# Two heads in one PSUM bank: both casts first, then both subtractions

## The chip, the cores and the metric

The kernel runs on one core of one Trainium2 chip. The metric is the time of one execution on the device in microseconds (us), less is better. The engines of the core work from queues of their own, each in its own order: TensorE (PE, matrix products and transposes), VectorE (DVE), ScalarE (ACT), GpSimd (POOL) and SyncE (SP, which here issues transfers). PSUM is the memory that TensorE writes its results to, in eight banks of 512 fp32 columns by 128 rows.

## The reference

One decoder layer on x of 1024 tokens by 1024 features. Two groups of eight heads (64 wide) read one input projection: group A with a sliding window of 128, two key heads, ALiBi and sinks; group B with forget gates over all earlier tokens. Then an output projection with a residual, and an MLP with squared ReLU.

```python
xn = rmsnorm(x, attn_norm_g)
proj = jnp.einsum('bsd,de->bse', xn, w_in)
qa, ka, va, qb, kb, vb, f_logit = jnp.split(proj, IN_SPLITS, axis=-1)
qa = rmsnorm(qa.reshape(b, s, A_HEADS, HEAD_DIM), q_norm_a)     # ka, qb, kb alike
out_a = swa_sinks_attention(qa, ka, va, sink_logits)
log_f = jax.nn.log_sigmoid(f_logit + b_forget)
out_b = forgetting_attention(qb, kb, vb, log_f)
x = x + jnp.einsum('bse,ed->bsd', mixed, w_out)
hid = jnp.square(jax.nn.relu(jnp.einsum('bsd,df->bsf', rmsnorm(x, mlp_norm_g), w_up)))
x = x + jnp.einsum('bsf,fd->bsd', hid, w_down)
```

## The kernel before, in words

Products are made from numbers split in two parts. A high part is the number cast to the matmul's shorter fp32 form (type fp32r), a low part is what the cast left over; a product is then the sum of two or three passes. Usually ScalarE casts the high part, and VectorE or GpSimd subtracts to get the low part.

*Stages.* Up to about 45 us x and the first weights are loaded and split, and the first projection runs (tile qps). From 45 to 200 us follow the other projections of group A (tile ps) and group A's attention; from there to about 430 us group B's four pairs of heads, with the next pair's projection (ps) or the first half of the output projection (tile po) as filler between the attention's small products. Then the output projection ends, and the MLP takes the rest: the up products (pu) to about 770 us, the down products (pd) to the end.

*Turned banks.* Projected and normalised queries and keys lie with tokens along the rows. `turn` (line 327) transposes four blocks of 128 tokens on TensorE into one PSUM bank (tiles ptq for queries, ptk for keys, from a ring of three banks that the probabilities' transposes, tpa and tpb, share). The bank then holds head features along the rows: two heads, one in rows 0 to 63 and the other in rows 64 to 127. `rows_of` gives each head's rows.

From the bank, each head's part is made into high and low parts:

- Queries: `q_split` (lines 321 to 325) has ScalarE cast with a gain (line 322) and VectorE multiply and subtract (line 323). The high part goes to the head's own rows of q1a or q1b, the low part to the other 64 rows of the same tile. `make_q_a` (line 347) serves group A, `make_q_b` (line 355) group B, both head by head.
- Keys: `k_split` (lines 369 to 376) has ScalarE copy the high part twice, to both row halves of k1a or k1b (lines 371 and 372), and VectorE make the low part k2z (line 374), for group A twice. `make_k_a` (line 380) does this for the two key heads in one bank, `make_k_b` (line 388) for one head at a time.

*Who reads them.* Scores (`scores_a`, `scores_b`) are TensorE products of q1a or q1b with k1 and then k2z, into tiles sp and spb (two banks in turn). VectorE adds the bias and takes the row minimum (lines 543 and 717), ScalarE the exponential (lines 550 and 722). Probabilities are transposed (lines 564 and 762), split by ScalarE and VectorE (lines 401 and 402), and multiplied with the values (pv, pvb). The mix is added up (lines 575 and 780) and stored by SP.

*Other work on the same queues.* ScalarE also copies finished projections out of PSUM (lines 458, 459 and 646, from a ring of two banks) and casts weights (line 76). VectorE also multiplies earlier mixes with their inverse sums (line 623), once a transfer has brought these.

*The order of the work.* The source gives dependencies and priorities; `prep` raises the priority of the attention's steps over the filler. The kernel is built with

```python
with tile.TileContext(nc, schedule_with_timeline_sim=True) as tc:
```

so a planner works out, from modelled times, the order in which each engine gets its instructions, and adds the waits between engines. 
Of the kernel before, what the change touches and what calls it, by code (L numbers as in the profile page):

```python
# [8 lines left out]
F32 = mybir.dt.float32  # L9
F32R = mybir.dt.float32r  # L10
BF16 = mybir.dt.bfloat16
AF = mybir.ActivationFunctionType
ALU = mybir.AluOpType
# [8 lines left out]
HD = 64  # L22
# [32 lines left out]
def hybrid_layer(  # L55
# [13 lines left out]
    nc = tc.nc  # L69
# [11 lines left out]
    def rsqrt(pool, out, t, shape, tag):  # L81
# [15 lines left out]
        out=ident, in_=ident, pattern=[[-1, P]], compare_op=ALU.not_equal,  # L97
# [12 lines left out]
    gqk = cp.tile([P, 2], F32, name="gqk")  # L110
# [42 lines left out]
    def x_part(j, k, rows):  # L153

        c, r0 = divmod(rows.start, 512)
        return X[c][k // 2][:, j, k % 2, r0 : r0 + rows.stop - rows.start]
# [27 lines left out]
    for k in range(KT):  # L184
# [18 lines left out]
        for cs in pieces:  # L203
            hi, lo = (x_part(j, k, cs) for j in range(2))
            nc.scalar.activation(hi, xr[:, cs], AF.Copy, scale=ga)
            last_x = nc.vector.scalar_tensor_tensor(  # L206
                out=lo, in0=xr[:, cs], scalar=ga,
                in1=hi.bitcast(F32), op0=ALU.mult, op1=ALU.subtract,
# [109 lines left out]
        )  # L318
        return v

    def q_split(hi, lo, src, gain):
        nc.scalar.activation(hi, src, AF.Copy, scale=gain)
        nc.vector.scalar_tensor_tensor(
            out=lo, in0=src, scalar=gain, in1=hi.bitcast(F32), op0=ALU.mult, op1=ALU.subtract
        )

    def turn(x, col, w, c, name):
        pt = pa.tile([P, 512], F32, tag="tr", name=name, bufs=3)
        for j in range(4):
            nc.tensor.transpose(  # L330
                pt[:w, j * P : (j + 1) * P], x[:, 4 * c + j, col : col + w], ident
            )
        return pt
# [7 lines left out]
    rows_of = [slice(h * HD, (h + 1) * HD) for h in range(2)]  # L341
# [5 lines left out]
    def make_q_a(g, c, j):  # L347
        x, col = (((q0, 0), (q3, 0)), ((q3, P), (q3, 2 * P)))[g][j]
        q1 = qa[g, j, c]
        pt = turn(x, col, P, c, "ptq")  # L350
        for h in range(2):
            r, ro = rows_of[h], rows_of[1 - h]
            q_split(q1[r, h, :], q1[ro, h, :], pt[r, :], gqk[r, 0:1])

    def make_q_b(x, p):
        q1 = [ap2.tile([P, S], F32R, tag="q1", name=f"q1b{p}{h}", bufs=4) for h in range(2)]
        for c in range(2):
            cs = slice(c * 512, (c + 1) * 512)
            pt = turn(x, 0, P, c, "ptq")
            for h in range(2):  # L360
                r, ro = rows_of[h], rows_of[1 - h]
                q_split(q1[h][r, cs], q1[h][ro, cs], pt[r, :], gqk[r, 1:2])
        return q1

    k2_of = [ap2.tile([P, S], F32R, name=f"k2z{i}") for i in range(2)]

    def k_split(k1, i, src, cs, both):
        r, ro = rows_of[i], rows_of[1 - i]  # L370
        nc.scalar.copy(k1[r, cs], src)
        nc.scalar.copy(k1[ro, cs], src)
        for rr in (r, ro) if both else (r,):
            nc.vector.tensor_tensor(
                out=k2_of[i][rr, cs], in0=src, in1=k1[r, cs].bitcast(F32), op=ALU.subtract
            )

    k1a = {}

    def make_k_a(x, col, c):  # L380
        cs = slice(c * 512, (c + 1) * 512)
        pt = turn(x, col, P, c, "ptk")
        for g in range(2):
            if c == 0:
                k1a[g] = ap2.tile([P, S], F32R, tag="k1", name=f"k1a{g}", bufs=2)
            k_split(k1a[g], g, pt[rows_of[g], :], cs, True)

    def make_k_b(x, col, p, h):
        k1 = ap2.tile([P, S], F32R, tag="k1", name=f"k1b{p}{h}", bufs=2)
        if p == 0:  # L390
            nc.gpsimd.memset(k2_of[h][rows_of[1 - h], :].bitcast(F32), 0.0)
        for c in range(2):
            cs = slice(c * 512, (c + 1) * 512)
            pt = turn(x, col + h * HD, HD, c, "ptk")
            k_split(k1, h, pt[:HD, :], cs, False)
        return k1

    def evict_pt(pt, cols):
# [11 lines left out]
    for t in range(NT):  # L410
# [4 lines left out]
        out=rt, in0=rt, scalar1=1.0 / D, scalar2=EPS, op0=ALU.mult, op1=ALU.add  # L415
# [6 lines left out]
    for t in range(0, NT, 4):  # L422
# [8 lines left out]
        out=dist, in_=dist, pattern=[[-1, 256]], compare_op=ALU.is_ge, fill=BIG,  # L431
# [3 lines left out]
        out=dist, in_=dist, pattern=[[1, 256]], compare_op=ALU.is_ge, fill=BIG,  # L435
# [8 lines left out]
    for pattern, base, sign in (  # L444
# [5 lines left out]
            out=before, in_=before, pattern=pattern, compare_op=ALU.is_ge, fill=0.0,  # L450
# [58 lines left out]
    def start_a():  # L509
        for c in range(2):  # L510
            tiles_q_a(0, c)
        for t in range(2):
            wa1_tile(t)
        for c in range(2):
            wa1_tile(2 + c)
            with tc.issue_after(middle[-1]):
                prep(make_k_a, q0, P, c)
            prep(make_q_a, 0, c, 0)
        for g in range(2):
            va.append(split_v(q0[:, :, 256 + g * HD : 256 + (g + 1) * HD], f"va{g}"))  # L520
        prep(make_q_a, 0, 0, 1)
        for t in range(4, NT):
            wa1_tile(t)
        prep(make_q_a, 0, 1, 1)
# [130 lines left out]
    def prep_q(p):  # L655
        heads[p, "q"] = make_q_b(qkb[p], p)

    def prep_k(p, h):
        heads[p, "k1", h] = make_k_b(qkb[p], P, p, h)
        if h == 0:  # L660
            load_c(p, 0)
# [343 lines left out]
    rr = o["zr"].tile([P, S], F32, name="rr")  # L1005
# [231 lines left out]
    queued, both = [], []  # L1237
# [175 lines left out]
    for i in range(len(STEPS)):  # L1413
        down(i)
        if STEPS[i][0] == len(PHASES) - 1 and late:
            name, dt, cs = late.pop(0)
# [65 lines left out]
```

## Time and profile before

| | |
|---|---|
| three runs, median | 1080.25 us (1079.21 to 1080.84) |
| the profiled execution's own time | 1080.32 us |
| its span, first to last instruction | 1078.6 us |
| TensorE busy | 1069.6 us, 99% |
| VectorE busy | 774.6 us, 72% |
| ScalarE busy | 575.6 us, 53% |
| GpSimd busy | 382.0 us, 35% |
| granted TensorE clock | 1.000 |

The span leaves out 1.72 us of the execution's time around the first and last instruction. Busy shares are means over all stages. A wait in the profile is given with the instruction that ended it: "PE sp L72 <- DVE q1a L323" reads: TensorE stood before its product into sp, called at line 72, until VectorE had written q1a at line 323. The `mm` helper makes all products at line 72, so they are told apart by their tiles.

### The profile page before, as it was taken

What the parts mean: (1) busy time and instruction counts of PE and PEld (TensorE: products, weight loads), DVE (VectorE), ACT (ScalarE), POOL (GpSimd) and SP (SyncE); (2) the same over time, 40 slices, a digit from 0 to 9 for tenths busy, and PEclk for the clock granted to TensorE, in tenths of its full rate; (3) what the DMA queues carried; (4) which work ended last, traced back from release to release, by engine and by line L of the source; (5) the groups of instructions that cost most, each with busy time, mean ns of one, the idle gap of its engine ahead of it and who ended that gap; (6) DMA issues with size and microseconds to landing.
All of it is one profiled execution on the core that took longest, in us unless ns stands there. A gap on an engine that the chain in (4) does not pass through costs nothing.

```text
span 1078.6 us, 15605 instructions
## 1 busy us (share of the span) xinstructions
PE 1069.6 (99%) x5506; PEld 931.9 (86%) x5506; DVE 774.6 (72%) x1319; ACT 575.6 (53%) x1024; POOL 382.0 (35%) x347
## 2 busy tenths in 40 slices
PE   9999999999999999999999999999999999999998
PEld 8999999999998888888888888888888888888887
DVE  7377787777775777997877869674775876764395
ACT  5558587777666765555445454534533433333331
POOL 5572423546456663333233322332212313231100
PEclk9999999999999999999999999999999999999999
DMA  9402111424657665645554543443998886665423
GB/s 285 169 16 60 61 44 57 122 79 148 224 192 241 218 226 217 205 156 176 185 175 178 178 173 120 178 162 117 372 391 308 306 294 207 243 220 184 172 92 117
DMA packets 96366, 195.93 MB, mean 182 GB/s; under 512 B 7408, under 2 KB 19872, under 8 KB 96288
## 3 DMA queue, kind: packets, MB, share of 16 engines
q1 hardware_dynamic: 96000, 194.80, 52.0%
q8 instruction: 43, 0.70, 0.3%
q14 instruction: 35, 0.29, 0.1%
q10 hardware_dynamic: 288, 0.15, 0.0%
HBM read 141.87 MB, written 53.04 MB: 181 GB/s over the span
## 4 chain that ended last, share of the span: by engine, by line
PE 90%; DVE 3%; DMA 2%; ACT 2%; POOL 1%; issue 1%; SPq 0%; DVEq 0%; ACTq 0%; POOLq 0%
PE pu L72 28%; PE pd L72 28%; PE ps L72 12%; PE po L72 8%; PE spb L72 3%; PE pvb L72 3%; PE tpb L762 2%; PE sp L72 1%; PE pv L72 1%; PE tpa L564 1%; DMA xq<-in_x_dram 1%; DVE x L206 1%; PE ptk L330 1%; DMA wr<-in_w_a_dram 1%; PE ptq L330 0%
## 5 line engine op out<-in xcount | busy, mean ns | idle before, releaser
L72 PE MATMUL pd<-hx,wx 128*128 128x512 f32 (+1 forms) x1356 | 305.0, 387 | 0.0
L72 PEld LDWEIGHTS pd<-hx,wx 128*128 128x128 f32 x1356 | 253.1, 188 | 51.9
L72 PE MATMUL pu<-bh,wu 128*128 128x512 f32 x896 | 276.1, 389 | 0.0
L72 PE MATMUL ps<-w,x 128*128 128x384 f32 (+1 forms) x960 | 198.5, 343 | 0.8 <-ACT qkb L646 0.5
L72 PEld LDWEIGHTS pu<-bh,wu 128*128 128x128 f32 x896 | 168.2, 188 | 34.9
L72 PE MATMUL pu<-bl,wu 128*128 128x512 f32 x448 | 174.1, 389 | 0.0
L72 PEld LDWEIGHTS ps<-w,x 128*128 128x128 f32 x960 | 165.3, 188 | 5.1 <-ACT qkb L646 0.7
L76 ACT CAST hx<-hr 128x1024 fp32r<-128x1024 f32 x56 | 59.1, 1054 | 175.8 <-PE pd L72 171.1
L79 POOL TENSOR_TENSOR wx<-wda,wx 128x1024 fp32r<-128x1024 f32 x24 | 65.6, 2731 | 195.4 <-ACT wx L76 168.9
L79 DVE TENSOR_TENSOR hx<-hr,hx 128x1024 fp32r<-128x1024 f32 x56 | 72.3, 1300 | 71.5 <-ACT hx L76 71.5
L72 PEld LDWEIGHTS pu<-bl,wu 128*128 128x128 f32 x448 | 84.1, 188 | 17.6
L72 PE MATMUL po<-mix,wos 128*128 128x512 f32 x384 | 94.4, 394 | 0.1
L79 POOL TENSOR_TENSOR wu<-wus,wu 128x512 fp32r<-128x512 f32 x31 | 44.8, 1447 | 112.4 <-ACT wu L76 112.4
L72 PEld LDWEIGHTS po<-mix,wos 128*128 128x128 f32 x384 | 70.7, 188 | 14.0 <-ACT pc L950 0.3
L79 POOL TENSOR_TENSOR wu<-wur,wu 128x512 fp32r<-128x512 f32 x31 | 44.8, 1447 | 98.8 <-ACT wu L76 84.5
L76 ACT CAST wu<-wus 128x512 fp32r<-128x512 f32 x64 | 38.4, 618 | 62.8 <-PE pu L72 55.9
L1071 DVE TENSOR_TENSOR ht<-hb 128x512 f32<-128x512 f32 x32 | 21.7, 720 | 59.4 <-ACT hb L1182 59.4
L76 ACT CAST wx<-wda 128x1024 fp32r<-128x1024 f32 x56 | 58.5, 1049 | 7.2 <-DMA wda<-in_w_d_dram 7.2
L402 DVE TENSOR_TENSOR ptl<-tpb,pth 128x512 fp32r<-128x512 f32 (+1 forms) x80 | 49.7, 632 | 15.1 <-ACT pth L401 14.5
L722 ACT ACTIVATE sb<-sb,nmb 128x128 f32<-128x128 f32 (+3 forms) x64 | 49.8, 778 | 19.7 <-DVE nmb L717 19.1
L79 POOL TENSOR_TENSOR w<-wr,w 128x384 fp32r<-128x384 f32 (+1 forms) x47 | 50.1, 1078 | 27.7 <-ACT w L76 15.0
L401 ACT CAST pth<-tpb 128x512 fp32r<-128x512 f32 (+1 forms) x80 | 42.3, 544 | 14.3 <-PE pvb L72 6.2
(211 smaller groups left out, 1789.1 us busy)
## 6 DMA issues: line engine op xcount, KB each, us to landing
wda<-in_w_d_dram SPq DMA_DIRECT2D x34, 1024.0 KB, 9.1
hr<-hid_d SPq DMA_DIRECT2D x56, 512.0 KB, 6.3
wur<-in_w_u_dram SPq DMA_DIRECT2D x32, 512.0 KB, 4.4
hid_d<-ht SPq DMA_DIRECT2D x16, 1024.0 KB, 4.3
hid_d<-hb SPq DMA_DIRECT2D x16, 768.0 KB, 3.8
mix<-mixs_d SPq DMA_DIRECT2D x7, 1024.0 KB, 6.2
wr<-in_w_b_dram SPq DMA_DIRECT2D x32, 192.0 KB, 2.4
xq<-in_x_dram SPq DMA_DIRECT2D x8, 512.0 KB, 5.7
```

The source lines that it names most:

```text
L72: return nc.tensor.matmul(out, lhsT, rhs, start=start, stop=stop)
L76: hi_eng.copy(hi, src)
L79: return lo_eng.tensor_tensor(out=lo, in0=src, in1=hi.bitcast(F32), op=ALU.subtract)
L206: last_x = nc.vector.scalar_tensor_tensor(out=lo, in0=xr[:, cs], scalar=ga, in1=hi.bitcast(F32), op0=ALU.mult, op1=ALU.subtract,)
L330: nc.tensor.transpose(pt[:w, j * P : (j + 1) * P], x[:, 4 * c + j, col : col + w], ident)
L401: nc.scalar.copy(hi[:, cols], pt[:, cols])
L402: nc.vector.tensor_tensor(out=lo[:, cols], in0=pt[:, cols], in1=hi[:, cols].bitcast(F32), op=ALU.subtract)
L564: nc.tensor.transpose(tp[:, hh * P : (hh + 1) * P], pts[hh // 2][:, hh % 2, c0 : c0 + P], ident)
L722: nc.scalar.activation(pr[:, :nk], pr[:, :nk], AF.Exp, scale=-1.0, bias=nm[:, c : c + 1], accum_out=dn_b[p % 2][:, h, i : i + 1] if p < 3 ...
L762: nc.tensor.transpose(tp[:, c0 : c0 + P], probs[qi][:, kb * P : (kb + 1) * P], ident)
L1071: eng.tensor_tensor(out=out, in0=a, in1=b, op=ALU.subtract)
```

## The change

Both queries' and keys' helpers take all heads of a bank at once. ScalarE's casts of all heads come first in the source, then VectorE's subtractions of all heads. What each instruction reads and writes stays the same.

```diff
-    def q_split(hi, lo, src, gain):
-        nc.scalar.activation(hi, src, AF.Copy, scale=gain)
-        nc.vector.scalar_tensor_tensor(
-            out=lo, in0=src, scalar=gain, in1=hi.bitcast(F32), op0=ALU.mult, op1=ALU.subtract
-        )
+    def q_splits(pt, gain, plane):
+
+        rr = [(rows_of[h], rows_of[1 - h]) for h in range(2)]
+        for h, (r, _) in enumerate(rr):
+            nc.scalar.activation(plane(h)[r], pt[r, :], AF.Copy, scale=gain[r])
+        for h, (r, ro) in enumerate(rr):
+            nc.vector.scalar_tensor_tensor(
+                out=plane(h)[ro], in0=pt[r, :], scalar=gain[r],
+                in1=plane(h)[r].bitcast(F32), op0=ALU.mult, op1=ALU.subtract,
+            )
...
     def make_q_a(g, c, j):
...
-        for h in range(2):
-            r, ro = rows_of[h], rows_of[1 - h]
-            q_split(q1[r, h, :], q1[ro, h, :], pt[r, :], gqk[r, 0:1])
+        q_splits(pt, gqk[:, 0:1], lambda h: q1[:, h, :])
...
     def make_q_b(x, p):
...
-            for h in range(2):
-                r, ro = rows_of[h], rows_of[1 - h]
-                q_split(q1[h][r, cs], q1[h][ro, cs], pt[r, :], gqk[r, 1:2])
+            q_splits(pt, gqk[:, 1:2], lambda h: q1[h][:, cs])
...
-    def k_split(k1, i, src, cs, both):
-        r, ro = rows_of[i], rows_of[1 - i]
-        nc.scalar.copy(k1[r, cs], src)
-        nc.scalar.copy(k1[ro, cs], src)
-        for rr in (r, ro) if both else (r,):
-            nc.vector.tensor_tensor(
-                out=k2_of[i][rr, cs], in0=src, in1=k1[r, cs].bitcast(F32), op=ALU.subtract
-            )
+    def k_splits(parts, cs, both):
+        for k1, i, src in parts:
+            for rr in rows_of[i], rows_of[1 - i]:
+                nc.scalar.copy(k1[rr, cs], src)
+        for k1, i, src in parts:
+            r, ro = rows_of[i], rows_of[1 - i]
+            for rr in (r, ro) if both else (r,):
+                nc.vector.tensor_tensor(
+                    out=k2_of[i][rr, cs], in0=src, in1=k1[r, cs].bitcast(F32), op=ALU.subtract
+                )
...
     def make_k_a(x, col, c):
...
-            k_split(k1a[g], g, pt[rows_of[g], :], cs, True)
+        k_splits([(k1a[g], g, pt[rows_of[g], :]) for g in range(2)], cs, True)
...
     def make_k_b(x, col, p, h):
...
-            k_split(k1, h, pt[:HD, :], cs, False)
+            k_splits([(k1, h, pt[:HD, :])], cs, False)
```

## The prediction

> **What bounds the kernel now.** I read the page first, then the busy time by stage, then the waits of TensorE alone, and last the timeline around the turned banks.
>
> ```profile
> span 1078.6 us, 15605 instructions
> PE 1069.6 (99%) x5506; PEld 931.9 (86%) x5506; DVE 774.6 (72%) x1319; ACT 575.6 (53%) x1024; POOL 382.0 (35%) x347
> ```
>
> TensorE (PE) is busy for 1069.6 of 1078.6 us. Whatever ScalarE (ACT) and VectorE (DVE) save counts only where TensorE stands still for it. The turned banks are made between 45 and 430 us, so that stretch is cut by stages:
>
> ```profile
> core 0: us, PE busy (x) PEld busy (x) DVE busy (x) ACT busy (x) POOL busy (x), PEclk, DMA share, GB/s
> 45.00:75.00 30.00, 29.45 (x173) 28.46 (x172) 20.21 (x44) 14.08 (x38) 20.03 (x24) 1.00 0.00 1
> 75.00:110.00 35.00, 34.54 (x224) 33.07 (x224) 26.59 (x81) 28.89 (x85) 14.18 (x16) 1.00 0.20 58
> ...
> 200.00:250.00 50.00, 49.64 (x332) 47.81 (x331) 36.11 (x92) 34.96 (x76) 20.77 (x29) 1.00 0.36 103
> 250.00:290.00 40.00, 39.49 (x266) 38.32 (x265) 29.86 (x66) 29.70 (x65) 24.75 (x29) 1.00 0.53 158
> ...
> 330.00:380.00 50.00, 49.89 (x300) 43.43 (x299) 33.11 (x78) 36.56 (x74) 33.24 (x36) 1.00 0.69 229
> 380.00:430.00 50.00, 48.54 (x300) 42.15 (x299) 36.68 (x88) 31.84 (x71) 22.17 (x24) 1.00 0.62 220
> ...
> 470.00:760.00 290.00, 290.00 (x1281) 240.11 (x1280) 213.84 (x300) 138.49 (x178) 89.66 (x62) 1.00 0.45 161
> ```
>
> The columns are the stretch, its length, then each engine's busy time. TensorE is short of full by 0.55, 0.46, 0.36, 0.51, 0.11 and 1.46 us in the six attention rows: 3.45 us, of which 1.99 us lie before 380 us. From 470 us on no stage holds anything of the change. So 3.45 us, 0.32% of the time, is the most that this view lets any reordering here win.
>
> [...]
>
> What TensorE waited for, over the whole span (total, times, longest, in us):
>
> ```profile
> PE tpb L762 <- DVE ptl L402: 1.3, 3, 0.6
> PE qps L72 <- DVE warm L180: 1.3, 1, 1.3
> PE ps L72 <- ACT qkb L646: 0.5, 1, 0.5
> PE qps L72 <- ACT x L205: 0.5, 1, 0.5
> PE sp L72 <- DVE nm_a L543: 0.5, 1, 0.5
> PE pv L72 <- DVE mta L575: 0.4, 1, 0.4
> PE sp L72 <- DVE q1a L323: 0.3, 1, 0.3
> PE ps L72 <- ACT z L459: 0.3, 1, 0.3
> ```
>
> One row alone names a line of the change: 0.3 us for q1a, written at line 323.
>
> **The change part by part.** It adds and removes no instruction, no transfer and no buffer. SP and POOL get nothing new and nothing is moved past their queues. Per turned bank it moves the second head's ScalarE cast ahead of the first head's VectorE subtraction. Today the two engines take turns on one bank; here are bank and both heads of the first query half of a pair:
>
> ```profile
> 160.60 0.68 ACT L322 ACTIVATE q1b<-ptq,gqk 64x512 fp32r<-64x512 f32 x1
> ...
> 161.37 0.73 DVE L323 SCALAR_TENSOR_TENSOR q1b<-ptq,gqk,q1b 64x512 fp32r<-64x512 f32 x1
> ...
> 162.14 0.69 ACT L322 ACTIVATE q1b<-ptq,gqk 64x512 fp32r<-64x512 f32 x1 [0.50 <-DVE q1b L323]
> ...
> 164.48 0.76 DVE L323 SCALAR_TENSOR_TENSOR q1b<-ptq,gqk,q1b 64x512 fp32r<-64x512 f32 x1
> ```
>
> The second cast shares no data with the first subtraction, only the bank, and yet it waits 0.50 us for it. So accesses of different engines to one bank are kept in source order, and the edit turns cast, subtract, cast, subtract (three handovers) into cast, cast, subtract, subtract (one).
>
> [...]
>
> Durations, and what the banks cost the two engines in waits (min/median/max in ns; waits as total us, times):
>
> ```profile
> L322 ACT ACTIVATE q1b<-ptq,gqk x16: 676/684/692, 160.6 to 340.9; 64x512 fp32r<-64x512 f32 x16
> L323 DVE SCALAR_TENSOR_TENSOR q1b<-ptq,gqk,q1b x16: 735/750/757, 161.4 to 341.7; 64x512 fp32r<-64x512 f32 x16
> ...
>   DVE q1b L323: 4.5, 6
>   DVE q1a L323: 4.1, 4
> ...
> L374 DVE TENSOR_TENSOR k2z<-ptk,k1a x8: 673/689/695, 55.7 to 67.5; 64x512 fp32r<-64x512 f32 x8
> L371 ACT CAST k1a<-ptk x4: 563/577/583, 53.2 to 65.2; 64x512 fp32r<-64x512 f32 x4
> ...
> ACT k1a L371 <- DVE k2z L374: 5.0, 2, 3.5
> ```
>
> *Which banks.* 16 query casts at two per bank give 8 banks for q1b, and q1a has as many: 16 query banks. The key banks with two heads are the two of group A (k1a, 4 casts at line 371). The 16 banks of k1b pass one head only, and for them the edit changes nothing.
>
> *Busy time.* Unchanged: 0.684 us per query cast, 0.750 per query subtraction, whatever the order. Alone on idle engines a query bank takes 2 x 0.684 + 2 x 0.750 = 2.87 us plus the handovers, which are 0.09 us (160.60 + 0.68 to 161.37) and 0.04 (161.37 + 0.73 to 162.14) here. Two fewer save about 0.1 us per bank, in latency and not in TensorE time. Covered: TensorE has projection matmuls from the same stage to run, and it stands still at one of the 18 banks now.
>
> *ScalarE's waits go.* 5.0 us for k2z, and the 0.50 us quoted above for q1b. What they hold up on ScalarE's queue is seen at the group A keys:
>
> ```profile
> 57.10 0.58 ACT L371 CAST k1a<-ptk 64x512 fp32r<-64x512 f32 x1 [1.54 <-DVE k2z L374]
> 57.62 0.74 DVE L323 SCALAR_TENSOR_TENSOR q1a<-ptq,gqk,q1a 64x512 fp32r<-64x512 f32 x1
> ...
> 58.42 0.39 PE L72 MATMUL sp<-k1a,q1a 128*128 128x256 f32 x1 [0.28 <-DVE q1a L323]
> ...
> 65.24 0.58 ACT L371 CAST k1a<-ptk 64x512 fp32r<-64x512 f32 x1 [3.46 <-DVE k2z L374]
> ...
> 67.93 0.28 ACT L459 ACTIVATE z<-ps,rstd 128x8 f32<-128x8 f32 x1
> 68.26 3.12 PE L72 MATMUL ps<-w,x 128*128 128x392 f32 x16 [0.28 <-ACT z L459]
> ```
>
> Both TensorE waits stand behind such a ScalarE wait: the 0.28 us at 58.42 follows the 1.54 us at 57.10, and the 0.28 us at 68.26 is for a bank whose copies (q, then z) queue behind the casts that start 3.46 us late. With four casts in a row the casts no longer wait, and both stalls can go. That is -0.56 us; lower end of the gain 0 (the next thing, the q1a subtraction behind four k2z subtractions of 0.689 us, is late instead), upper end 1.99 us, all idle time before 380 us. I take -0.56, the two rows that hang on the edit.
>
> *VectorE waits longer once.* The first subtraction of a bank now waits for both casts: 0.684 us later for 16 query banks and 2 x 0.577 = 1.15 us for two key banks, 16 x 0.684 + 2 x 1.15 = 13.2 us in all if nothing covers it. Behind it on VectorE queue the score reductions (lines 543 and 717, which free the score banks for TensorE), the low parts of probabilities (line 402, which TensorE's products read) and the mix additions (lines 575 and 780, ahead of the stores to mix_d on SP). Against that, the wait of the second subtraction goes. How much of a VectorE wait reaches TensorE: today VectorE stands 4.5 + 4.1 = 8.6 us for these casts and TensorE lost 0.28 us to line 323, 3%. At that rate 13.2 us cost 0.4 us. Below, the end is 0, or a gain if the second waits weigh more; above, 13.2 us if all of it came through. I take 0, because the order on each engine is written by a planner that models these waits and puts other ready work into them, and because the second wait's loss works the other way; 0.4 stays for the range.
>
> *What does not go.* The wait on the qkb copy hangs on a transfer:
>
> ```profile
> 275.26 0.90 DVE L623 TENSOR_TENSOR mixr<-mixr,mixn 128x512 f32<-128x512 f32 x1 [1.99 <-DMA mixn<-rd_d]
> ...
> 276.25 0.62 ACT L76 CAST mixn<-mixr 128x512 fp32r<-128x512 f32 x1 [2.78 <-DVE mixr L623]
> ...
> 277.30 0.80 PE L72 MATMUL ps<-w,x 128*128 128x384 f32 x3 [0.51 <-ACT qkb L646]
> ```
>
> A query bank lies right beside it, but the copy waits behind the mixn cast, which waits for VectorE, which waits for the load: 0.51 us stay. So do the 1.46 us after 380 us: the last query cast is at 340.9 us, and what stands there is mostly the 1.3 us for line 402.
>
> *Sum.* -0.56 + 0 = -0.56 us. The profiled execution took 1080.32 us (1.72 more than its span) and the median of the runs is 1080.25, 0.07 below it. 1080.32 - 0.56 gives 1079.76, or 1079.69 from the median: I predict 1079.7. Less than 0.2%, 2.2 us, cannot be told from no change by a measurement of this kernel.
>
> **The rivals.**
>
> *No effect: the planner orders the engines as before, or the waits are not of the bank's order.* For it: many banks already show little wait (10 of 32 VectorE instructions at line 323 waited). Against it: the 3.46 us at 65.24, where the second group's cast waits for the first group's subtractions. Time 1080.3.
>
> *Faster: the order is drawn anew, and well.* The planner works out each engine's order from modelled times, so ScalarE's earlier casts shift everything behind them. If all 1.99 us before 380 us went and half of the 1.46 after it, 2.7 us, the time would be 1077.6. For it: ScalarE's 5.0 us sit at the start of the stage, upstream of everything. Against: it takes 64% (2.2 of 3.45 us) of the idle time to show at all, and the largest stalls are for line 402 and the transfer, which the edit does not touch.
>
> *Slower: the wait of the first subtraction takes the place of ScalarE's.* Place: the head of VectorE's queue at the 18 banks, with score reductions behind it. VectorE is busy 26.59 of 35 us and 36.11 of 50 us in these stages, so a stand of 0.7 us often finds something waiting. Price: at a quarter of 13.2 us coming through, 3.3 - 0.56 = 2.7 us, time 1083.0. It decides when (2.2 + 0.56) / 13.2 = 21% comes through, seven times today's 3%.
>
> **How the numbers follow.** The forecast (two stalls gone, nothing else) 0.38, no effect 0.13: together 0.51 within 0.2%. Faster 0.24, slower 0.25. A slower outcome gets as much as a faster one, since idle time caps the gain at 3.45 us and nothing caps a loss. The range goes from a little past the faster rival, 1077.3, to the slower rival, 1083.0, and leaves about 1 in 10 out on each side. The likeliest case's own range is 1078.3 (1.99 us gained) to 1080.7 (0.4 us lost).
>
> **What would show it.** Right: of a query bank, two ScalarE casts in succession and then two subtractions; the waits of ScalarE on k2z (5.0 us) gone; the TensorE waits on q1a at line 323 and on z at line 459 gone from the list; busy times as before; 470 to 760 us as full as now. VectorE's wait on the casts of line 322 would stay near 8.6 us. Wrong: TensorE idle in 45 to 430 us over 5.6 us, with new rows that name lines 543, 717 or 402; or that idle time under 1.3 us. If the time moves and the idle time of TensorE does not, the loss is in the interleaving of its instructions, and my reading of the busy share is at fault.

## The result, and the profile after

The changed kernel takes 1087.72 us (median of 4 runs, 1086.49 to 1088.95), the kernel before 1079.88 us on the same chip: 1.0074 times as long, 95% interval 1.0061 to 1.0086. It is slower by 0.74%, 7.8 us. I had forecast 1079.7 us, with 1077.3 to 1083.0 as the range.

The page of the changed kernel, the first two lines that matter:

```profile
span 1085.9 us, 15623 instructions
PE 1072.7 (99%) x5506; PEld 931.7 (86%) x5506; DVE 775.2 (71%) x1319; ACT 574.4 (53%) x1024; POOL 382.0 (35%) x347
```

The work is the same: TensorE has the same 5506 products, VectorE 775.2 us against 774.6, ScalarE 574.4 against 575.6. Of the 7.3 us of span, 4.2 show as idle time of TensorE (13.2 us instead of 9.0) and 3.1 as busy time (1072.7 instead of 1069.6). No product was added, so the second part is not work. A product of 512 columns by itself shows 0.39 us (the first up product below), while in a row they start 0.23 us apart (58 in 13.46 us, last section): by my estimate from these two figures, a standstill of up to about 0.16 us counts as busy. So idle time is a lower bound of what TensorE stood still, and I read the 3.1 us as standstill too. Busy time by stage, in the same stretches as before:

```profile
core 0: us, PE busy (x) PEld busy (x) DVE busy (x) ACT busy (x) POOL busy (x), PEclk, DMA share, GB/s
...
75.00:110.00 35.00, 33.98 (x216) 32.12 (x215) 26.76 (x82) 28.27 (x83) 13.73 (x15) 1.00 0.20 58
...
150.00:200.00 50.00, 49.22 (x307) 45.71 (x306) 35.20 (x100) 37.78 (x95) 22.24 (x27) 1.00 0.21 61
200.00:250.00 50.00, 49.34 (x325) 46.87 (x325) 36.95 (x90) 34.66 (x75) 17.44 (x25) 1.00 0.29 94
250.00:290.00 40.00, 37.80 (x255) 36.16 (x254) 30.59 (x66) 28.41 (x65) 25.45 (x29) 1.00 0.52 162
...
330.00:380.00 50.00, 48.91 (x293) 42.28 (x292) 34.95 (x83) 36.56 (x77) 31.21 (x35) 1.00 0.62 213
380.00:430.00 50.00, 49.22 (x302) 42.48 (x301) 33.97 (x86) 31.85 (x69) 26.64 (x26) 1.00 0.65 224
```

TensorE's idle time in these six rows is 1.02, 0.78, 0.66, 2.20, 1.09 and 0.78 us, 6.5 us in all. Before, they held 0.46, 0, 0.36, 0.51, 0.11 and 1.46 us, 2.9 us. The idle time that is new lies after 150 us, and most of it at 250 to 290 us; at 75 to 110 us there is 0.56 us more, but the 0.55 us of 45 to 75 us are gone. What TensorE waited for (total us, times, longest):

```profile
PE tpb L765 <- DVE q1b L327: 1.5, 2, 1.1
...
PE tpb L765 <- DVE ptl L405: 1.2, 3, 0.4
PE spb L72 <- DVE nmb L720: 1.1, 3, 0.7
PE pd L72 <- DVE hx L79: 0.8, 1, 0.8
PE pvb L72 <- DVE ptl L405: 0.6, 1, 0.6
PE tpa L567 <- DVE k2z L377: 0.6, 2, 0.3
PE sp L72 <- DVE q1a L327: 0.6, 1, 0.6
PE tpb L765 <- DVE rd L590: 0.4, 1, 0.4
```

No single wait makes the loss. Two rows name the pairs' subtraction (line 327, 2.1 us together). The others name score reductions (720), low parts of probabilities (405), inverse sums (590), and k2z of banks that hold one head only (377, at 189.7 and 191.2 us). The longest of all, in the timeline:

```profile
278.75 0.83 DVE L626 TENSOR_TENSOR mixr<-mixr,mixn 128x512 f32<-128x512 f32 x1 [0.45 <-DMA mixn<-rd_d]
...
279.62 1.51 DVE L327 SCALAR_TENSOR_TENSOR q1b<-ptq,gqk,q1b 64x512 fp32r<-64x512 f32 x2
...
281.27 0.63 PE L765 MATMUL tpb<-ident,sb 128*128 128x128 f32 x4 [1.06 <-DVE q1b L327]
```

Two subtractions (x2, 1.51 us) run one after the other, behind a VectorE multiplication that waited 0.45 us for a transfer. The transposes of probabilities want the bank that they release and stand 1.06 us. Read alone, this looks like the cause of the loss. The experiments below say that it is not.

To measure the attention by itself I use the start of the first up product (tile pu), which follows the whole stretch. Before, then changed:

```profile
464.43 0.39 PE L72 MATMUL pu<-bh,wu 128*128 128x512 f32 x1
```

```profile
469.72 0.39 PE L72 MATMUL pu<-bh,wu 128*128 128x512 f32 x1
```

So 5.3 of the 7.3 us are lost before the up products. Another 2.0 us are lost after their start, most of them in the down products (last section).

### The profile page after: what moved, and what is told of

Same layout as the page of the kernel before. It is cut to its first block, busy times and chain, and to the rows that moved or that the text cites. A ratio compares the mean times of both kernels' runs of the same rounds, so it can differ in the third digit from the quotient of the medians.

```text
span 1085.9 us, 15623 instructions
## 1 busy us (share of the span) xinstructions
PE 1072.7 (99%) x5506; PEld 931.7 (86%) x5506; DVE 775.2 (71%) x1319; ACT 574.4 (53%) x1024; POOL 382.0 (35%) x347
## 4 chain that ended last, share of the span: by engine, by line
PE 63%; DMA 3%; DVE 2%; ACT 1%; issue 0%; SPq 0%; POOL 0%; DVEq 0%; ACTq 0%; POOLq 0%
PE pu L72 28%; PE pd L72 25%; PE po L72 7%; PE pvb L72 1%; PE tpb L765 1%; DMA hr<-hid_d 1%; DMA wda<-in_w_d_dram 1%; PE spb L72 1%; DMA wor<-in_w_o_dram 1%; DMA xt<-in_xT_dram 0%; DVE hx L79 0%; DVE wx L79 0%; DMA part_d<-xt 0%; DVE ptl L405 0%; DVE wda L1074 0%
## 5 line engine op out<-in xcount | busy, mean ns | idle before, releaser
L72 PE MATMUL ps<-w,x 128*128 128x384 f32 (+1 forms) x960 | 193.3, 341 | 0.0
L715 POOL TENSOR_SCALAR_AFFINE_SELECT cm<-cb 128x128 f32<-128x128 f32 (+1 forms) x64 | 31.0, 485 | 58.3 <-DVE nmb L720 50.4
```

The lines of the kernel that those rows point to most:

```text
L72: return nc.tensor.matmul(out, lhsT, rhs, start=start, stop=stop)
L715: nc.gpsimd.affine_select(out=cm, in_=bias, pattern=[[-1, n]], compare_op=ALU.is_ge, fill=BIG, base=n - P, channel_multiplier=1,)
```

## The experiments

Theory P: the loss sits in the pair itself. VectorE waits for two casts, then holds its queue and the bank for two subtractions, and TensorE waits behind it. Theory R: the pair shifts a few modelled times, the planner draws another order for all engines, and that order costs the time, wherever it was set off.

"Rows moved" below is a rough measure of what differs in the written order: each engine's instructions in the order that the built program has them, with line and buffer numbers left out and runs of equal instructions taken as one row. Of TensorE's 2604 rows before, it is the number that stand in one list and not the other. In the changed kernel that is 743. The column "in the trace" takes the order in which TensorE's products and transposes ran instead (1877 rows before), and counts the rows that stand in one list or the other. The two counts differ in size, but part the kernels in the same way: four that nearly keep the order, and the rest. The first up product is from one profiled execution of each kernel.

| kernel | rows moved | in the trace | first up product, us | ratio to before, 95% interval |
|---|---|---|---|---|
| other subtraction twice (e6) | 12 | 4 | 463.90 | 1.0010, 1.0001 to 1.0019 |
| second key bank paired (e7) | 16 | 4 | 465.17 | 1.0005, 0.9996 to 1.0014 |
| heads reversed (e4) | 87 | 33 | 464.21 | 1.0007, 0.9998 to 1.0015 |
| 4 query banks of A paired (e8) | 93 | 22 | 464.93 | 1.0011, 1.0002 to 1.0020 |
| 8 query banks of B paired (e1) | 522 | 709 | 464.22 | 1.0014, 1.0004 to 1.0024 |
| 16 query banks paired (e10) | 681 | 716 | 466.18 | 1.0024, 1.0015 to 1.0034 |
| 8 query banks of A paired (e2) | 657 | 468 | 466.79 | 1.0027, 1.0016 to 1.0038 |
| changed, one subtraction twice (e11) | 718 | 735 | 466.50 | 1.0038, 1.0025 to 1.0050 |
| two key banks of A paired (e3) | 683 | 887 | 471.26 | 1.0069, 1.0054 to 1.0084 |
| one query bank paired (e9) | 672 | 884 | 469.30 | 1.0073, 1.0058 to 1.0089 |
| changed | 743 | 767 | 469.72 | 1.0074, 1.0061 to 1.0086 |
| changed, another one twice (e12) | as changed, but for 6 | 767 | 469.44 | 1.0074, 1.0061 to 1.0087 |
| one subtraction twice (e5) | 669 | 883 | 471.94 | 1.0077, 1.0064 to 1.0091 |

**The parts alone.** Only the named helper takes both heads at once; all else is as before.

```diff
 # e1, make_q_b only
+q_splits(pt, gqk[:, 1:2], lambda h: q1[h][:, cs])
 # e2, make_q_a only
+q_splits(pt, gqk[:, 0:1], lambda h: q1[:, h, :])
 # e3, make_k_a only
+k_splits([(k1a[g], g, pt[rows_of[g], :]) for g in range(2)], cs, True)
```

> Only the 8 query banks of group B are made in pairs; group A's queries and keys head by head as before. Theory P (the loss sits in the pair itself: VectorE stands for two casts and then holds its queue for two subtractions, and TensorE waits behind it): since the changed kernel loses its 5.3 us between 160 and 430 us, where only group B's banks lie, nearly all of it is here, 1084 to 1086 us. Theory R (the loss comes from a newly drawn order of all engines, whichever bank started it): anything from 1079 to 1088 us, with new stalls also at places that have no turned query bank near them.

> Only the 8 query banks of group A (54 to 145 us in the profile before) are made in pairs. Theory P: a loss can only arise before 150 us; the changed kernel was 0.3 to 0.7 us ahead there, so 1079 to 1081 us and the TensorE stalls after 150 us as before. Theory R: the order is drawn anew after 150 us too, the stalls there differ from before, and the time lies anywhere from 1078 to 1087 us.

> Only the two key banks of group A (53 to 68 us) are made in pairs. Theory P: two stalls of 0.3 us go, 1079 to 1080 us, and everything after 150 us as before. Theory R: new stalls after 150 us, hundreds of us behind the only edit, and a time that may be several us from before.

P fell here. Group B's eight banks, beside which the stalls of the changed kernel lie, cost 0.14%, and TensorE reaches the up products at 464.22 us, 0.2 us earlier than before: in its profile nothing is lost in the attention, and the loss is in the down products (last section). The two key banks, made at 50 to 68 us, cost 0.69% alone. The three parts add up to 1.1%, the whole costs 0.74%.

**Another order of heads.**

```diff
-for h in range(2):
+for h in (1, 0):          # make_q_a and make_q_b, head by head
```

> Head by head as before, but the head in rows 64 to 127 first in all 16 query banks: same handovers, same waits, another order. Theory P: no pair, no loss, 1079 to 1081 us. Theory R: the order of all engines is drawn anew as well, so stalls elsewhere change and the time may move by 1 to several us either way.

1.0007, not told from 1. I had expected under R that any edit draws a new order; this one moves 87 rows only. So the edit as such is not enough: it takes one that sends the planner another way.

**Added work that draws a new order, and added work that does not.** In the kernel before, one subtraction into k2z is made twice, for either key head of the second key bank.

```diff
 k_split(k1a[g], g, pt[rows_of[g], :], cs, True)
+if (c, g) == (1, 0):      # e5; (1, 1) in e6
+    nc.vector.tensor_tensor(
+        out=k2_of[g][rows_of[1 - g], cs], in0=pt[rows_of[g], :],
+        in1=k1a[g][rows_of[g], cs].bitcast(F32), op=ALU.subtract)
```

> No pair at all: head by head as before, but one VectorE subtraction (the copy of k2z in the other rows, first key head, second key bank, 0.69 us) is made twice, with the same result. In the written order of the engines this one instruction moves 669 of TensorE's 2604 rows, and leaves an order that differs from that of the kernel with paired key banks alone by 18 rows. Theory R (the order drawn costs the time, not the pair): as with the paired key banks alone, 1085 to 1088 us, with TensorE stalls at 250 to 290 and 330 to 380 us. Theory P (the pair costs it): one more 0.69 us on an engine that is not the bound, 1079.5 to 1081 us.

> The control: the same VectorE subtraction made twice for the second key head of the same bank. The same added work, but the written order of TensorE differs from before by 12 rows only. Both theories: 1079.5 to 1081 us; a loss like that of the sibling would mean that the added subtraction itself costs the time, and would speak against R.

This decides between the two. Neither kernel has a pair, both have the same added 0.69 us on VectorE. The one whose order moves loses 0.77%, the other 0.10%. The first has almost the order of the paired key banks (18 rows apart, 4 in the traces), and TensorE's longer waits are the same. Its waits, then those of the paired key banks:

```profile
PE tpb L767 <- DVE ptl L407: 1.7, 3, 0.9
...
PE pvb L72 <- ACT pth L406: 1.0, 1, 1.0
PE spb L72 <- DVE nmb L722: 0.7, 1, 0.7
```

```profile
PE tpb L784 <- DVE ptl L424: 1.7, 3, 0.9
...
PE pvb L72 <- ACT pth L423: 1.1, 1, 1.1
...
PE spb L72 <- DVE nmb L739: 0.7, 1, 0.7
```

Different edits, one order, the same stalls (the lines are shifted by the edits), 200 to 360 us behind the edit: the 0.9 us end at 281.4 us with the paired key banks and at 283.1 us here, the 1.1 and 1.0 us at 346.5 and 347.1 us.

**Pairs with the order kept.**

```diff
 # e7, make_k_a: in pairs for c == 1, head by head for c == 0
 # e8, make_q_a: in pairs for g == 0, head by head for g == 1
```

> Only the second key bank of group A is made in a pair (the one at which ScalarE waited 3.46 us). TensorE's written order differs from before by 16 rows, where both key banks together moved 683. Theory R: the order is kept, so no loss, and the stall for the copy at line 459 may go: 1079 to 1080.5 us. Theory P: at least half of the 7 us of the two key banks, 1083 to 1087 us.

> The four query banks of group A's first key head (54 to 77 us) are made in pairs; TensorE's written order differs from before by 93 rows. All eight of group A cost 0.27%. Theory R: order nearly kept, 1079 to 1081 us, no stall changed after 150 us. Theory P: half of it, about 1081.5 us, with the loss near the banks, before 110 us.

Where the order is kept, the paired second key bank costs nothing that can be told: 1.0005, against the 1.003 or more that P asked for. The four query banks do not part the theories: 1.0011 (1.0002 to 1.0020) holds both R's time and P's, and is about what e6 loses without any pair. Neither kernel gains. The copy at line 459 that TensorE waited for is gone from the waits of the paired second key bank, but what TensorE waits for is others:

```profile
PE sp L72 <- DVE q1a L323: 1.4, 2, 1.1
...
PE ps L72 <- POOL w L79: 0.9, 1, 0.9
```

**One pair, all query pairs, and the changed kernel with its order flipped.**

```diff
 # e9, make_q_a: in pairs for (g, c, j) == (0, 1, 0), head by head elsewhere
 # e10: the changed kernel with make_k_a head by head
 # e11, e12: the changed kernel, after k_splits in make_k_a:
+if c == 1:                # e11; c == 0 in e12
+    nc.vector.tensor_tensor(
+        out=k2_of[0][rows_of[1], cs], in0=pt[rows_of[0], :],
+        in1=k1a[0][rows_of[0], cs].bitcast(F32), op=ALU.subtract)
```

> One single query bank of the 18 is made in a pair (group A, first key head, second half of the tokens). By the written orders it lands on the order of the kernel with one subtraction made twice and of the one with paired key banks (47 rows of TensorE differ from the latter, 672 from before). Theory R: 1085 to 1088 us from one bank. Theory P: one eighteenth of the loss, 1080 to 1081 us.

> All 16 query banks in pairs, group A's key banks head by head. Its order differs from before by 681 rows of TensorE, and from the changed kernel's by about as many. Theory P: the sum of the two query parts, 0.14 + 0.27 = 0.4%, 1084 us. Theory R: an order of its own, 1079 to 1088 us, not bound to that sum.

> All 18 banks in pairs as in the changed kernel, with one VectorE subtraction of the second key bank made twice (0.69 us, the same result). This flips the written order (731 rows of TensorE from the changed kernel) to nearly that of the kernel with paired queries alone (77 rows). Theory R: the time of that kernel, whichever it is, and not the changed kernel's; if that one is faster, then added work makes the changed kernel faster. Theory P: the changed kernel's time or slightly more, 1087 to 1089 us.

> The control: as the sibling, but the subtraction made twice is one of the first key bank, and the written order stays that of the changed kernel but for 6 rows of TensorE. Both theories: the changed kernel's time, 1086.5 to 1089 us.

One bank of 18 in a pair costs as much as all 18; it lands on the order of the paired key banks (47 rows apart, 27 in the traces), and TensorE's 0.9 and 1.1 us are there too, up to 280.1 and 344.5 us. Sixteen query pairs cost 0.24%, a third of the changed kernel, and about what group A's eight cost alone. And the changed kernel gets faster when it is given more work: with one subtraction twice 1.0038 instead of 1.0074, the intervals apart. The control with the order kept stays at 1.0074. In the flipped kernel, still with all 18 pairs, no row names line 327; its largest wait is at the fourth turned query bank, at 78.3 us, for GpSimd:

```profile
PE ptq L335 <- POOL q L309: 1.6, 1, 1.6
```

Grouped by order, the times agree within their intervals: e3, e5 and e9 1.0069 to 1.0077; the changed kernel and e12 1.0074 both (no row apart in the traces); e10 and e11 1.0024 and 1.0038 (25 rows apart), with the up products begun at 466.18 and 466.50 us. Kernels of up to 93 rows moved lie within 0.11% of before, those of 522 and more between 0.14 and 0.77% above. How many rows move does not set the price: e1 moves 522 and loses nothing in the attention, e10 moves 681 and e3 683, and e10 loses a third of what e3 does. None is faster than before.

## Why the prediction was right or wrong

*What bounds the kernel* was right. Only the idle time was taken too strictly: the 3.45 us were no cap, since by the estimate above (0.39 less 0.23 us) short standstills count as busy. TensorE is busy 99% of the span in both kernels, and VectorE (+0.6 us), ScalarE (-1.2 us) and GpSimd (-0.1 us) have no more to do than before: the loss is in when their results come.

*ScalarE's waits go, -0.56 us*: half right. The 5.0 us of ScalarE for k2z have no row left in the changed kernel. But the two TensorE stalls that I hung on them came back: 0.6 us for q1a where there were 0.3, and 0.3 us for the z copy (now ahead of a score product). The gain was 0 at best, the low end that I named. With the order kept (e7) it was not there either: there TensorE's longest wait in the attention is for q1a, up to 79.6 us.

*VectorE waits longer once, 0*: VectorE's own waits came out about as forecast, what they cost TensorE did not. VectorE waited 3.9 us for casts into q1a and 3.8 for q1b, 7.7 in all, against my "near 8.6". TensorE's loss to line 327 rose from 0.3 to 2.1 us, 27% of that, where I had taken today's 3%. By this row alone the "slower" rival would look right, but e11 has the same 18 pairs and none of it: the order sets it, not the pair alone. The sign that I had named for "wrong" came too: 6.5 us idle in six stages, over the 5.6, with rows for the score reductions and the low parts (now 720 and 405).

*Same bank, source order*: the trace of the changed kernel agrees. The casts come as two (x2, 1.38 us at 279.55 us), the subtractions as two, and none of the pairs' casts waits for a subtraction. So the rival "no effect" was wrong too.

*The step that failed* is one sentence: the VectorE term was put at 0 "because the order on each engine is written by a planner that models these waits and puts other ready work into them". I used the planner as cover, and did not price what it costs when it draws another order. My "faster" rival had the order drawn anew, and only as a gain; the "slower" rival took its price from waits beside the banks, 1083.0 us at most. The runs give the price: 0.24 to 0.77% for four orders (e2's, that of e10 and e11, that of e3, e5 and e9, and the changed kernel's) that one bank, one repeated subtraction, or two to eighteen pairs set off, and nothing in the attention for e1's. In the changed kernel it is 5.3 us up to the first up product, where the forecast had -0.56. No row before gave this size; the direction could be read: 385 us of attention in which the planner has to keep TensorE fed, with only 3.45 us idle, so a new order had little left to gain and much to lose, and the range should have reached further up. The other 2.0 us of the loss lie behind the attention and are not explained (last section).

What is argued and not shown is why these orders wait more. That the planner's modelled times differ from the chip's, so that an order good in the model meets late VectorE and ScalarE results, fits the mixed waits, but no run separates it from an order that is worse in the model as well.

## What to carry to other kernels

Under a planner, the first question about a small edit is whether it moves the order: compare each engine's written order before and after, and only then look at the mechanism. When a loss shows up far from the edit, add idle work that does the same to the order without the mechanism (a result computed twice), with a control that keeps the order; these two runs told the cause here. A stall that names your edited line is not proof: here the longest one named it, and it went away with all the pairs in place.

## What the runs showed of the hardware

In the kernel with paired key banks a half-busy stretch had a slower clock behind it. TensorE is busy for only 2.11 of 4 us at 76 to 80 us, and the granted clock in the next 4 us is 0.57 (the third number from the end, ahead of the share and the rate of the DMA):

```profile
76.00:80.00 4.00, 2.11 (x13) 1.35 (x11) 3.22 (x12) 2.73 (x10) 3.99 (x5) 1.00 0.26 81
80.00:84.00 4.00, 4.00 (x16) 3.90 (x17) 2.72 (x10) 3.79 (x15) 2.28 (x3) 0.57 0.42 121
```

Cut closer to the drop, TensorE is busy for 1.75 of 3.30 us, and then the clock is 0.50:

```profile
77.10:80.40 3.30, 1.75 (x10) 1.37 (x11) 3.27 (x13) 2.19 (x10) 2.89 (x4) 1.00 0.39 121
80.50:83.80 3.30, 3.30 (x14) 3.20 (x12) 2.22 (x8) 3.29 (x13) 2.08 (x3) 0.50 0.37 113
```

In that stretch nine products of 384 columns take 3.08 us, where the kernel before runs ten in 1.90 us at about the same place:

```profile
80.54 3.08 PE L72 MATMUL ps<-w,x 128*128 128x384 f32 x9
```

```profile
79.61 1.90 PE L72 MATMUL ps<-w,x 128*128 128x384 f32 x10
```

Nine at 0.19 us would be 1.71, so by this estimate the slower clock adds 1.4 us to 1.9 us of idle time. The same kernel has a second stretch at a slower clock at 282 to 286 us (0.59), with TensorE busy for 1.12 of the 2 us ahead of it. In the kernel before the stretch 76 to 80 us was busy 3.54 of 4 us, and the clock at 80 to 84 us stayed at 1.00. No long standstill stood ahead of the drop at 80 us: TensorE's longest wait there was 0.9 us, in a stretch about half busy. A stretch like that doesn't always have a slower clock behind it. In e11 (the changed kernel with one subtraction twice) TensorE is as little busy at 75 to 78.3 us, and the clock stays at 1.00:

```profile
75.00:78.30 3.30, 1.68 (x10) 1.35 (x8) 2.81 (x5) 3.24 (x9) 2.67 (x4) 1.00 0.05 7
78.40:81.70 3.30, 3.01 (x17) 2.33 (x18) 3.23 (x14) 2.38 (x12) 3.30 (x4) 1.00 0.28 90
```

What parts the two is open. The profiled run of the changed kernel has no stretch at a slower clock (1.00 in all of its rows above), and its span is 7.3 us longer than before, against 7.1 us with the paired key banks. With the paired key banks, two of the six executions had a mean granted clock of 1.000, and took 1084.97 and 1086.59 us, still 5 us and more above before; the others, at 0.995 to 0.998, took 1086.50 to 1091.42. So the clock is a share of some orders' loss and not the cause.

The down products of the changed kernel lose 1.7 us more, from about 895 to 920 us. There a VectorE subtraction took 3.42 us, where the one ahead of it, of the same shape, took 1.22:

```profile
897.10 1.22 DVE L79 TENSOR_TENSOR hx<-hr,hx 128x1024 fp32r<-128x1024 f32 x1
897.63 2.94 POOL L79 TENSOR_TENSOR wx<-wda,wx 128x1024 fp32r<-128x1024 f32 x1 [8.39 <-ACT wx L76]
898.23 3.42 DVE L79 TENSOR_TENSOR wx<-wda,wx 128x1024 fp32r<-128x1024 f32 x1
...
918.85 13.46 PE L72 MATMUL pd<-hx,wx 128*128 128x512 f32 x58 [0.76 <-DVE hx L79]
```

It starts while GpSimd works (897.63 to 900.57 us) and ends 1.08 us after GpSimd does; where GpSimd has nothing to do, at 1061 to 1069 us, such subtractions take 1.21 to 1.23 us. The one ahead of it started 0.53 us before GpSimd and took its 1.22 us. In the kernel before, two that start while GpSimd works (826.87 and 848.87 us) took 3.42 us as well, and end 1.08 us after it. I read these rows so that VectorE hardly moved on with such a subtraction until GpSimd was through. Kernels e1, e2 and e12 show about this loss in the down products too, e3, e5 and e9 none. A new order there is not its cause: in all the kernels the down products have the same written order on TensorE, VectorE, ScalarE and GpSimd, and in all the traces TensorE's last 2618 products run in the same order. Whether the loss belongs to the kernel or to the single execution was not tried.
